# One decoder step on one core: high part of the first weight ahead of a layer-norm boundary, residual behind it, and low parts ahead of the pivot in the output projections

## The chip, the cores and the metric

The kernel runs on one core of one Trainium2 chip. The metric is the device time of one execution in microseconds (us); the figures are medians of several runs. Engines are named as in the profile: PE is TensorE, DVE is VectorE, ACT is ScalarE, POOL is GpSimd, SP is the engine that issues most DMAs.

## The reference

The reference is one inference step of a decoder with two layers for 256 prompt tokens and 8 samples of 4 tokens (288 columns in the kernel, width 1024). Each layer is a half-step SwiGLU feed-forward, a token mixer (gated linear attention, GLA, in layer 0; dilated attention over a shared key/value cache in layer 1), and a second half-step feed-forward. Each of the six sub-layers ends in the same way:

```python
def modulate(x, shift, scale):
    return x * (1.0 + scale[:, None, :]) + shift[:, None, :]

def post_norm(x, y, gate, g, b):
    return layer_norm(ALPHA * x + (1.0 + gate[:, None, :]) * y, g, b)
```

The result of `post_norm` is used twice: modulated it is the input of the next projection, and times `ALPHA` it is the residual that the next `post_norm` adds. Shifts, scales and gates come from a product with the large weight `w_ada`.

## The kernel before, in words

**Products.** Activations lie with the width on partitions, as 8 chunks of 128 x 288. Every large product is made from three matmuls on values that are split into a high and a low part (`mm3`: hi by xh on L531, hi by xl on L532, lo by xh on L533). The tiles `xh` and `xl` are the split activation, `hi` and `lo` the split weight; in the key/value projection the activation is called `kh` and `kl`, and between the two halves of a feed-forward `hh` and `hl`.

**Weights.** The class `Stream` loads pieces of 512 KB in the fixed order of `job_list` by SP's queue into 11 buffers `raw`. A weight of 1024 x 256 is two pieces, called parts here. Each part is split when it is asked for (`part`, `split_part`): ACT copies it to `hi` (L177) and DVE subtracts to get `lo` (L179). `take` prepares one job more than it returns, `more(n)` prepares n further parts. Jobs of kind `ada` are the pieces of `w_ada`; `fill` runs them on PE (L450, with the transposes L466) between other work. `weave` spreads a list of ada jobs among weights: `lead` weights come first, and the ada jobs are spread over the rest of the first `span`.

**What sets the order.** A tile scheduler orders each engine's instructions, except that those given to `pin` keep their written order in a chain for each engine. Engines run their queue in order. The splits, the instructions of a boundary and the statistics are pinned, the residual is not.

**A boundary** is the work between two sub-layers. I write (l, s) for the one after sub-layer s of layer l; there are five, (0,0), (0,1), (0,2), (1,0) and (1,1), around 272, 472, 714, 1014 and 1334 us of the trace. First come the layer-norm statistics (`stats`, L617 to L645): sums over partitions by matmuls with `ones` (L623, L627), then DVE's variance and ACT's root. `spread` (L651) brings the factor to all partitions. Then `post_norm` goes over the chunks c = 0 to 7: DVE takes off the mean (`center`, L668; for c up to 2 inside `stats` and `spread`), `scaled` makes the modulated value `xm` on DVE (L758 for the prompt, L763 and L764 for the samples), ACT rounds it to `xh` (L760, L765), and one chunk later DVE makes `xl` (L767, L769). After c = 2 comes `S.more(1)`: one part of the weight that follows is split there, with `hi` on ACT and `lo` on DVE. PE runs `project_chunkwise` behind it: for each chunk the matmuls of four PSUM banks, as soon as that chunk's `xh` and `xl` are there; PE's order is fixed and has ada matmuls (L450) between the chunks.

**The residual** (`Post.residual`) is a generator: for each chunk DVE makes `ax` from `z` with a factor and `rstd` (L676), and POOL adds a bias (L678). It yields after every second chunk, and its caller decides in the text where the next two are emitted: in `ffn` ahead of step i = 1 to 5, in `gla` all that is left ahead of `wk`, in the dilated attention behind `post_norm`. Since L676 is not pinned, the scheduler places it: in the built program all eight stand within the boundary's chunks on DVE.

**The output projections** (`out_proj`, weights `wo` of layer 0 and `wob` of layer 1) take four weights of two chunks each. The first two weights give chunks 0 to 3 together. `Post.sublayer` makes `z` from the product, the gate and the residual (L570, L573, L575). With `late` = 4 a rough mean, the pivot (tile `lnpiv`, L588, from chunks 0 and 1), is subtracted: from `z` of chunks 0 to 3 by DVE (L602), and from the residual `ax` of chunks 4 to 7 by POOL (L595). `add` sums up `z` (L664, DVE here) and its squares (L665, POOL). Chunks 4 to 7 follow from weights 2 and 3; `S.more(3)` ahead of weight 3 splits three further parts.

**Rotation.** Behind boundary (1,0) stands the query projection (`wq` of layer 1), each of whose products ends in a rotation: ACT copies the PSUM bank in four quarters to `xm` (L1294), DVE multiplies out of the bank (L1295, tile `lnsq`; after it the bank is free), POOL multiplies `xm` (L1296), DVE adds both (L1298). There are four PSUM banks `pa` for all products.

## Time and profile before

| | |
|---|---|
| median of 3 runs | 1561.36 us (1559.15 to 1568.56) |
| profiled execution | 1566.59 us, its span 1564.5 us |
| mean granted TensorE clock | 0.98 |
| busy: PE, DVE, ACT, POOL | 95%, 59%, 46%, 14% of the span |
| chain that ended last: PE, DVE, ACT | 83%, 9%, 3% |

A row of the timeline gives start, duration, engine, line, operation, output<-inputs with their shape, and a count where neighbours are put together; in brackets stands the time that the engine was idle just before and what ended it. A row of the waits gives the waiting engine, tile and line, what it waited for, the total, how many times, and the longest. Starts of neighbouring instructions lie closer than their durations, since they overlap in the engine's pipeline; what an instruction takes from its queue is the distance to the next start.

### The profile page before, as it was taken

The page shows a single profiled execution, that of the slowest core. Times are in us where ns is not written, and L with a number is a line of the kernel's source. Part 1 is how long each engine was busy: PE and PEld are TensorE (multiplying, and loading weights), DVE is VectorE, ACT ScalarE, POOL GpSimd, SP SyncE. Part 2 cuts the span into 40 slices and gives each one's busy share as a digit, 9 for nine tenths or more (in the row PEclk, how much of TensorE's full clock was granted, in tenths as well). Part 3 has the DMA queues.
Part 4 walks back from the last instruction along what each step waited for, and adds up shares of the span by engine and source line. Part 5 has one row for each costly group of instructions (what it writes and reads, how often), then busy time and mean ns, then how long its engine had stood idle before and what let it go on. Part 6 is the DMA issues. An engine that isn't in the chain of part 4 may idle for free.

```text
span 1564.5 us, 31623 instructions
## 1 busy us (share of the span) xinstructions
PE 1487.1 (95%) x12706; PEld 1336.2 (85%) x12706; DVE 927.6 (59%) x2020; ACT 715.7 (46%) x1178; POOL 217.2 (14%) x312
## 2 busy tenths in 40 slices
PE   6999999999899999998999999999999989899996
PEld 4999998799778999998899999898766638899995
DVE  3644545596786444448745444675775667755455
ACT  2443434755744444346444433486543343444432
POOL 0000031201522000224100003232301002200001
PEclk8999999999999999999999999999998989999998
DMA  9977685636856767864566676767687997555520
GB/s 300 321 228 241 213 273 160 214 99 199 293 190 217 233 216 236 299 209 152 179 206 204 202 239 204 250 195 246 226 303 278 348 329 256 193 162 162 175 82 31
DMA packets 238420, 342.67 MB, mean 219 GB/s; under 512 B 12471, under 2 KB 201985, under 8 KB 238274
## 3 DMA queue, kind: packets, MB, share of 16 engines
q1 hardware_dynamic: 235810, 333.34, 64.7%
q0 software_dynamic: 2048, 7.14, 1.2%
q8 instruction: 99, 1.62, 0.4%
q14 instruction: 47, 0.39, 0.1%
q10 hardware_dynamic: 416, 0.17, 0.0%
HBM read 332.36 MB, written 8.26 MB: 218 GB/s over the span
## 4 chain that ended last, share of the span: by engine, by line
PE 83%; DVE 9%; ACT 3%; issue 2%; DMA 1%; POOL 0%; SPq 0%; DVEq 0%; ACTq 0%; POOLq 0%
PE pa L531 21%; PE pa L532 21%; PE pa L533 21%; PE pd L450 4%; PE pb L1381 4%; PE pa L1384 3%; PE pa L1381 2%; DVE lo L179 1%; PE pa L1042 1%; ACT pe L1407 1%; DVE xm L758 1%; DVE ax L676 1%; DMA xp<-in_x_prompt_dram 1%; ACT hi L177 0%; DVE lnacc L664 0%
## 5 line engine op out<-in xcount | busy, mean ns | idle before, releaser
L532 PE MATMUL pa<-xl,hi 128*128 128x288 f32 x1860 | 551.6, 298 | 6.8 <-DVE xl L769 6.8
L179 DVE TENSOR_TENSOR lo<-raw,hi 128x1024 fp32r<-128x1024 f32 x350 | 421.0, 1211 | 221.3 <-ACT hi L177 220.5
L533 PE MATMUL pa<-xh,lo 128*128 128x288 f32 x1860 | 547.6, 296 | 3.7 <-DVE lo L179 3.7
L531 PE MATMUL pa<-xh,hi 128*128 128x288 f32 x1860 | 543.5, 299 | 1.2 <-DVE lnsq L1295 0.8
L177 ACT ACTIVATE hi<-raw 128x1024 fp32r<-128x1024 f32 x350 | 358.7, 1035 | 260.6 <-PE pa L532 218.3
L532 PEld LDWEIGHTS pa<-xl,hi 128*128 128x128 f32 x1860 | 351.9, 189 | 14.0 <-DVE xl L769 9.4
L531 PEld LDWEIGHTS pa<-xh,hi 128*128 128x128 f32 x1860 | 347.9, 189 | 13.5 <-issue 10.0
L533 PEld LDWEIGHTS pa<-xh,lo 128*128 128x128 f32 x1860 | 351.7, 189 | 4.3 <-DVE lo L179 4.2
L531 PE MATMUL pa<-hh,hi 128*128 128x288 f32 x704 | 209.9, 298 | 0.0
L533 PE MATMUL pa<-hh,lo 128*128 128x288 f32 x704 | 208.1, 296 | 0.0
L532 PE MATMUL pa<-hl,hi 128*128 128x288 f32 x704 | 208.1, 296 | 0.0
L874 DVE TENSOR_TENSOR sa<-pa,sa 128x288 f32<-128x288 f32 x88 | 39.7, 454 | 179.9 <-PE pa L533 175.2
L531 PEld LDWEIGHTS pa<-hh,hi 128*128 128x128 f32 x704 | 132.6, 188 | 4.3 <-issue 2.9
L532 PEld LDWEIGHTS pa<-hl,hi 128*128 128x128 f32 x704 | 132.4, 188 | 0.2
L533 PEld LDWEIGHTS pa<-hh,lo 128*128 128x128 f32 x704 | 132.4, 188 | 0.1
L875 ACT ACTIVATE hh<-sa 128x288 fp32r<-128x288 f32 x88 | 38.7, 445 | 134.0 <-DVE sa L874 131.1
L873 ACT ACTIVATE sa<-pa 128x288 f32<-128x288 f32 x88 | 34.9, 401 | 93.6 <-PE pa L533 93.5
L450 PE MATMUL pd<-raw,cT 128*32 128x256 f32 x1008 | 73.3, 385 | 1.5 <-DMA raw<-in_w_ada_dram 1.4
L593 POOL TENSOR_TENSOR z<-z,lnpiv 128x288 f32<-128x288 f32 x6 | 4.7, 801 | 482.7 <-ACT lnpiv L588 482.7
L1384 PEld LDWEIGHTS pa<-ident,raw 128*128 128x128 f32 x448 | 49.7, 144 | 20.4 <-issue 9.4
L678 POOL TENSOR_SCALAR ax<-ax,lnba 128x288 f32<-128x288 f32 x40 | 54.9, 1376 | 71.3 <-DVE xm L764 69.4
L1384 PE MATMUL pa<-ident,raw 128*128 128x128 f32 x448 | 58.4, 282 | 5.4 <-ACT kt L1512 5.4
(380 smaller groups left out, 1761.4 us busy)
## 6 DMA issues: line engine op xcount, KB each, us to landing
raw<-in_w_ffn_up_dram SPq DMA_DIRECT2D x172, 512.0 KB, 4.8
raw<-in_w_ada_dram SPq DMA_DIRECT2D x110, 512.0 KB, 5.2
raw<-in_w_ffn_down_dram SPq DMA_DIRECT2D x80, 512.0 KB, 4.6
raw<-in_cache_k_dram SPq DMA_DIRECT2D x56, 512.0 KB, 6.7
raw<-in_cache_v_dram SPq DMA_DIRECT2D x56, 512.0 KB, 7.3
raw<-in_w_in_a_dram SPq DMA_DIRECT2D x24, 512.0 KB, 4.0
raw<-in_w_q_b_dram SPq DMA_DIRECT2D x24, 512.0 KB, 4.5
raw<-in_w_ada_dram SPq DMA_DIRECT2D x32, 256.0 KB, 5.8
```

The costliest lines, as they stand in the source:

```text
L177: self.pin("act", self.nc.scalar.activation(hv, src, AF.Copy))
L179: self.pin(low, eng.tensor_tensor(out=lo, in0=src, in1=hv.bitcast(F32), op=ALU.subtract))
L450: T.matmul(ps[32 * q:32 * q + 32, :], lhsT=cT[:, k, :], rhs=raw[kk][:, 256 * q:256 * q + 256], start=(k == 0), stop=(k == DC - 1), tile_po ...
L531: ins = [T.matmul(ps, lhsT=whi, rhs=xhi, start=first, stop=False), T.matmul(ps, lhsT=whi, rhs=xlo, start=False, stop=False), T.matmul(ps, ...
L532: T.matmul(ps, lhsT=whi, rhs=xlo, start=False, stop=False),
L533: T.matmul(ps, lhsT=wlo, rhs=xhi, start=False, stop=last)]
L678: G.tensor_scalar(out=ax[:, c, :], in0=ax[:, c, :], scalar1=bb_[:, c:c + 1], scalar2=None, op0=ALU.add)
L873: A.activation(sa, pa[:, 0:NT], AF.Silu)
L874: V.tensor_tensor(out=sa, in0=pu[:, 0:NT], in1=sa, op=ALU.mult)
L875: A.activation(hh[:, m, :], sa, AF.Copy)
L1381: pin("pe", T.matmul(*a, **k))
L1384: pin("pe", T.transpose(*a))
```

## The change

There are four parts.

First, `Stream.begin` splits one part in two steps: `hi` is emitted ahead of the first chunk of a boundary, and `lo` where `S.more(1)` stood, after c = 2. For that `split_part` returns the second step as a function.

Second, the residual's DVE instruction is pinned, so that it stays where the text emits it. In `ffn` that is ahead of steps 1 to 5. In `gla` the residual goes from ahead of `wk` to the four `wv` weights, two chunks at each. At (1,0) it is emitted behind `post_norm`, in one go.

Third, in the output projections `catch_up` does the pivot work of all chunks on DVE, for `z` of chunks 0 to 3 and for `ax` of chunks 4 to 7, and it is emitted when the third weight has been taken, which has its second low part split by then. POOL keeps no pivot work there.

Fourth, in the query projection of layer 1 the ada jobs start two weights later (`lead` 6 in place of 4) and are spread over the first 11 weights.

```diff
 class Stream:
-        self.split_part(self.split.setdefault(i, Weight()), self.jobs[i], self.raw.pop(x), f"{x}", low)
-        self.freed.add(x)
-        self.release()
-        return True
+        rest = self.split_part(self.split.setdefault(i, Weight()), self.jobs[i], self.raw.pop(x), f"{x}", low)
+
+        def end():
+            rest()
+            self.freed.add(x)
+            self.release()
+            return True
+
+        return end if low is None else end()
...
         self.pin("act", self.nc.scalar.activation(hv, src, AF.Copy))
-        eng = self.nc.vector if low == "dve" else self.nc.gpsimd
-        self.pin(low, eng.tensor_tensor(out=lo, in0=src, in1=hv.bitcast(F32), op=ALU.subtract))
         w.append([y.rearrange("p k (m c) -> p m k c", c=min(P, cols)) for y in (hv, lo)])
+
+        def rest():
+            self.pin("dve", self.nc.vector.tensor_tensor(out=lo, in0=src, in1=hv.bitcast(F32), op=ALU.subtract))
+
+        return rest
...
+    def begin(self):
+
+        self.pump()
+        end = self.part(None) if self.np < len(self.parts) else None
+        return end or (lambda: None)
...
-    jobs += weave(wq, adas((1, 6))[x:] + adas((1, 7)), lead=4) + ca + wob + adas((1, 8))[2:]
+    jobs += weave(wq, adas((1, 6))[x:] + adas((1, 7)), lead=6, span=11) + ca + wob + adas((1, 8))[2:]
...
 class Post:
-                    for q in range(self.late, DC):
-                        G.tensor_tensor(out=ax[:, q, :], in0=ax[:, q, :], in1=self.pivot, op=ALU.subtract)
+                    if self.late == 2:
+                        for q in range(2, DC):
+                            G.tensor_tensor(out=ax[:, q, :], in0=ax[:, q, :], in1=self.pivot, op=ALU.subtract)
...
             elif c < self.late:
-                if c == self.late - 1:
-                    for q in range(self.late):
-                        V.tensor_tensor(out=z[:, q, :], in0=z[:, q, :], in1=self.pivot, op=ALU.subtract)
-                        self.add(q)
+                pass
...
+        def catch_up(self):
+
+            for q in range(self.late):
+                V.tensor_tensor(out=z[:, q, :], in0=z[:, q, :], in1=self.pivot, op=ALU.subtract)
+                V.tensor_tensor(out=ax[:, self.late + q, :], in0=ax[:, self.late + q, :], in1=self.pivot, op=ALU.subtract)
+                self.add(q)
...
             for c in range(DC):
-                V.scalar_tensor_tensor(out=ax[:, c, :], in0=z[:, c, :], scalar=ga[:, c:c + 1], in1=rstd, op0=ALU.mult,
-                                       op1=ALU.mult)
+                pin("dve", V.scalar_tensor_tensor(out=ax[:, c, :], in0=z[:, c, :], scalar=ga[:, c:c + 1], in1=rstd,
+                                                  op0=ALU.mult, op1=ALU.mult))
...
     def post_norm(post, l, s, nxt):
         last, rs = None, None
+        low = S.begin()
         for c in range(DC):
...
             if c == 2:
-                S.more(1)
+                low()
...
     def out_proj(kind, g, xh, xl, tiles):
         for i in range(2, 4):
             w_ = S.take((kind, i))
+            if i == 2:
+                post.catch_up()
             if i == 3:
                 S.more(3)
...
     def gla(xh, xl, residual):
         qk("wq", qT, DK ** -0.5)
         for t in range(3):
             gates(t)
-        for _ in residual:
-            pass
         qk("wk", kT, 1.0)
...
         for i in range(4):
             w_ = S.take(("wv", i))
+            next(residual)
             for m in range(2):
                 p_ = bankA()
                 project(p_, w_, m, xh, xl)
```

The line numbers shift by 7 to 21: the residual is L695 and L697 after the change (L676 and L678 before), `lo` is L186 (L179), `center` L687 (L668), `xm` L777, L782 and L783 (L758, L763, L764), `xl` L786 and L788 (L767, L769), the rotation L1316, L1317 and L1319 (L1295, L1296, L1298), the pivot's subtraction L672 and L673 (L602, L595), and the sum L683 (L664).

The first place is DVE in boundary (0,1), from the split of a weight part behind chunk 2 on. Before, it reads:

```order
L179 TENSOR_TENSOR lo_5130<-raw_4858,hi_5129 128x1024
L668 TENSOR_TENSOR z<-z,pb_5004 128x288
L758 SCALAR_TENSOR_TENSOR xm_5136<-z,affs_4681,pb_5052 128x256
L763 TENSOR_TENSOR xm_5136<-z,rsS_5107 128x32
L676 SCALAR_TENSOR_TENSOR ax<-z,lnga_5309,lnacc_5103 128x288
L764 TENSOR_TENSOR xm_5136<-xm_5136,affb_4682 128x32
L767 SCALAR_TENSOR_TENSOR xl_5043<-xm_5121,affb_4682,xh_5042 128x256
```

Now it reads:

```order
L186 TENSOR_TENSOR lo_5105<-raw_4836,hi_5104 128x1024
L687 TENSOR_TENSOR z<-z,pb_5004 128x288
L777 SCALAR_TENSOR_TENSOR xm_5136<-z,affs_4681,pb_5052 128x256
L782 TENSOR_TENSOR xm_5136<-z,rsS_5110 128x32
L485 TENSOR_TENSOR mods<-pb_5609,bT 128x4x9
L783 TENSOR_TENSOR xm_5136<-xm_5136,affb_4682 128x32
L786 SCALAR_TENSOR_TENSOR xl_5043<-xm_5124,affb_4682,xh_5042 128x256
```

The residual's `ax` is gone from every chunk of the boundary, and a small ada instruction (L485) that stood ahead of `lo` now stands behind it. All eight `ax` stand behind the last `xl`, among the next feed-forward's steps.

The second place is DVE in the first output projection, from the third weight's first `lo` on (its second one is `lo_4861` before and `lo_4839` now). Before:

```order
L179 TENSOR_TENSOR lo_4855<-raw_4462,hi_4854 128x1024
L575 TENSOR_TENSOR z<-z,ax 128x32
L602 TENSOR_TENSOR z<-z,lnpiv_4822 128x288 x3
L664 TENSOR_TENSOR lnacc_4824<-z 128x288
L602 TENSOR_TENSOR z<-z,lnpiv_4822 128x288
L664 TENSOR_TENSOR lnacc_4824<-lnacc_4824,z 128x288
L179 TENSOR_TENSOR lo_4861<-raw_4544,hi_4860 128x1024
```

Now:

```order
L186 TENSOR_TENSOR lo_4833<-raw_4462,hi_4832 128x1024
L589 TENSOR_TENSOR z<-z,ax 128x32
L186 TENSOR_TENSOR lo_4839<-raw_4544,hi_4838 128x1024
L672 TENSOR_TENSOR z<-z,lnpiv_4822 128x288
L673 TENSOR_TENSOR ax<-ax,lnpiv_4822 128x288
L672 TENSOR_TENSOR z<-z,lnpiv_4822 128x288
L673 TENSOR_TENSOR ax<-ax,lnpiv_4822 128x288
L683 TENSOR_TENSOR lnacc_4824<-z 128x288
```

The second `lo` has gone ahead of six instructions, and the subtraction from `ax` has come to DVE from POOL.

The third place is DVE and POOL behind the last chunk of boundary (1,0). On DVE, before:

```order
L767 SCALAR_TENSOR_TENSOR xl_11005<-xm_11130,affb_10854,xh_11004 128x256
L769 TENSOR_TENSOR xl_11005<-xm_11130,xh_11004 128x32
L673 TENSOR_SCALAR lnga_15482<-gT 128x8
L674 TENSOR_SCALAR lnba_15483<-gT 128x8
L179 TENSOR_TENSOR lo_11162<-raw_10786,hi_11161 128x1024
L179 TENSOR_TENSOR lo_11168<-raw_10840,hi_11167 128x1024
L1295 TENSOR_TENSOR lnsq_11294<-pa_11173,ropeq_11143 128x288
```

On DVE, now:

```order
L786 SCALAR_TENSOR_TENSOR xl_11005<-xm_11130,affb_10854,xh_11004 128x256
L788 TENSOR_TENSOR xl_11005<-xm_11130,xh_11004 128x32
L186 TENSOR_TENSOR lo_11162<-raw_10786,hi_11161 128x1024
L186 TENSOR_TENSOR lo_11168<-raw_10840,hi_11167 128x1024
L695 SCALAR_TENSOR_TENSOR ax<-z,lnga_11273,lnacc_11061 128x288 x8
L1316 TENSOR_TENSOR lnsq_11294<-pa_11173,ropeq_11143 128x288
```

On POOL, now (before, all eight of the residual's stand in a row ahead of the first rotation):

```order
L1317 TENSOR_TENSOR xm_11293<-xm_11293,ropeq_11143 128x288
L697 TENSOR_SCALAR ax<-ax,lnba_11274 128x288 x2
L1317 TENSOR_TENSOR xm_11303<-xm_11303,ropeq_11143 128x288
L697 TENSOR_SCALAR ax<-ax,lnba_11274 128x288 x6
L1317 TENSOR_TENSOR xm_11313<-xm_11313,ropeq_11143 128x288
L1317 TENSOR_TENSOR xm_11323<-xm_11323,ropeq_11143 128x288
```

Here the residual is not interleaved with anything: all eight stand in one block on DVE between the low parts and the first rotation, and on POOL six of them stand ahead of the third rotation's product.

More of the change, by code (lines that the diff above doesn't have):

```diff
@@ L192, in prep, with more @@
             pass
-    def more(self, n, low="dve"):
+    def more(self, n):
         self.pump()
-        while n and self.np < len(self.parts) and self.part(low):
+        while n and self.np < len(self.parts) and self.part():
             n -= 1
+    def begin(self):
+        self.pump()
+        end = self.part(None) if self.np < len(self.parts) else None
+        return end or (lambda: None)
     def fill(self, limit=None):
@@ L848, in first_group @@
             for i in range(2):
-                S.split_part(w[i], jfirst[i], wfirst[i][:, k0:k0 + 4, :], f"f{i}{k0}")
+                S.split_part(w[i], jfirst[i], wfirst[i][:, k0:k0 + 4, :], f"f{i}{k0}")()
             if k0 == 0:
```

## The prediction

> **What bounds the kernel now.** I read the page first, for the engine that sets the time:
>
> ```profile
> span 1564.5 us, 31623 instructions
> PE 1487.1 (95%) x12706; PEld 1336.2 (85%) x12706; DVE 927.6 (59%) x2020; ACT 715.7 (46%) x1178; POOL 217.2 (14%) x312
> ```
>
> PE is busy for 95%, and the change neither adds nor removes a matmul. So all that it can win is time in which PE waits, and all that it can lose is a new wait of PE. Next I read the waits with PE as the engine, and kept the rows at the places that the change touches:
>
> ```profile
> PE pa L532 <- DVE xl L769: 6.8, 10, 2.2
> PE pa L533 <- DVE lo L179: 4.2, 3, 1.9
> PE pa L532 <- DVE kl L769: 2.8, 2, 2.0
> PE pb L623 <- DVE z L575: 2.6, 2, 1.3
> PE pa L531 <- DVE lnsq L1295: 1.9, 2, 1.2
> PE pd L450 <- DMA raw<-in_w_ada_dram: 1.4, 2, 0.7
> ```
>
> All but the last are waits for DVE: xl and kl in the boundaries, lo and z in the output projections, lnsq at the first rotation behind a boundary. The six rows add up to 19.7 us. That is the size of the whole stake, 1.3% of the span. Last I read the timeline at each of the places, for the order in which DVE came to be late.
>
> **Boundaries.** These are DVE's rows in boundary (0,1):
>
> ```profile
> 471.30 1.22 DVE L179 TENSOR_TENSOR lo<-raw,hi 128x1024 fp32r<-128x1024 f32 x1
> 472.43 0.45 DVE L668 TENSOR_TENSOR z<-z,pb 128x288 f32<-128x288 f32 x1
> 473.42 0.51 DVE L676 SCALAR_TENSOR_TENSOR ax<-z,lnga,lnacc 128x288 f32<-128x288 f32 x1
> 473.84 0.19 DVE L764 TENSOR_TENSOR xm<-xm,affb 128x32 f32<-128x32 f32 x1
> 474.44 0.45 DVE L668 TENSOR_TENSOR z<-z,pb 128x288 f32<-128x288 f32 x1
> 482.88 0.45 DVE L769 TENSOR_TENSOR xl<-xm,xh 128x32 fp32r<-128x32 f32 x1
> ```
>
> DVE needs 2.01 us for a chunk (472.43 to 474.44) without any idle time, and the residual's L676 takes 0.42 of it (473.42 to 473.84). Eight of them are 3.4 us, and three stand ahead of the `lo` of 471.30. PE's rows for the same stretch, and its longest waits in the other boundaries:
>
> ```profile
> 272.32 0.40 PE L551 MATMUL pa<-xl,hi 128*128 128x288 f32 x1 [0.45 <-DVE xl L769]
> 278.27 0.40 PE L532 MATMUL pa<-xl,hi 128*128 128x288 f32 x1 [0.96 <-DVE xl L769]
> ...
> 474.58 0.40 PE L532 MATMUL pa<-xl,hi 128*128 128x288 f32 x1 [2.15 <-DVE xl L769]
> 478.96 0.40 PE L532 MATMUL pa<-xl,hi 128*128 128x288 f32 x1
> 483.63 0.40 PE L532 MATMUL pa<-xl,hi 128*128 128x288 f32 x1
> ...
> 712.77 0.40 PE L532 MATMUL pa<-kl,hi 128*128 128x288 f32 x1 [0.79 <-DVE kl L769]
> 716.59 0.61 PE L532 MATMUL pa<-kl,hi 128*128 128x288 f32 x1 [1.96 <-DVE kl L769]
> ...
> 1332.39 0.40 PE L532 MATMUL pa<-xl,hi 128*128 128x288 f32 x1 [0.81 <-DVE xl L769]
> 1336.20 0.40 PE L532 MATMUL pa<-xl,hi 128*128 128x288 f32 x1 [1.96 <-DVE xl L769]
> ```
>
> In (0,1) PE waits 2.15 us at chunk 3, and DVE's last xl, ready at 483.33, comes 0.3 us before PE takes it at 483.63. Without the residual DVE is 1.3 us earlier at chunk 3 (three L676) and 3.4 earlier at the end. What is left of the wait at chunk 3 is 0.9; but the chunks behind it then come at 1.6 us each (2.01 less 0.42), and PE needs more than that. So the least gain is 1.3 (three L676 ahead of the wait) and the most 3.4 (all eight). I take 2.6, as the waits that PE shows in this stretch are hardly larger.
>
> In (0,0) and (0,2) the first part adds its own piece. There DVE waited for the high half:
>
> ```profile
> 274.97 1.23 DVE L179 TENSOR_TENSOR lo<-raw,hi 128x1024 fp32r<-128x1024 f32 x1 [0.57 <-ACT hi L177]
> ```
>
> ACT's copy now stands ahead of the first xh, in time that ACT spends waiting for xm. That takes 0.57 from DVE's path, and with three L676 DVE is 1.8 us earlier at chunk 3. In (0,0) the shown waits are 0.45 and 0.96, together 1.4. I take 1.4 (least 0.8, most 2.4). In (0,2) they are 0.79 and 1.96 and a smaller one. I take 2.6 (least 1.6, most 3.2). In (1,1) they are 0.81 and 1.96. I take 2.2 (least 1.3, most 2.8). Cover for the moved residual in the three boundaries that lead into feed-forward steps or into the keys and values is DVE's own idle time:
>
> ```profile
> sum 50.00, PE 50.00 PEld 48.57 DVE 24.40 ACT 22.59 POOL 0.00; mean PE 10.00 PEld 9.71 DVE 4.88 ACT 4.52 POOL 0.00
> ```
>
> This is the sum over 490 to 540 us in windows of 10 us, in the feed-forward behind (0,1): DVE is busy for half of it, and the eight add 3.4 us of 50. There I cost them at nothing; with the cover gone they would cost those 3.4 us. Boundary sum: 1.4 + 2.6 + 2.6 + 2.2 = 8.8 us.
>
> **Output projections.** Rows of DVE, then of POOL, then of PE in the first one:
>
> ```profile
> 444.18 3.08 DVE L602 TENSOR_TENSOR z<-z,lnpiv 128x288 f32<-128x288 f32 x3
> 448.16 0.45 DVE L602 TENSOR_TENSOR z<-z,lnpiv 128x288 f32<-128x288 f32 x1
> 449.52 1.81 DVE L179 TENSOR_TENSOR lo<-raw,hi 128x1024 fp32r<-128x1024 f32 x1
> ```
>
> ```profile
> 443.35 3.60 POOL L595 TENSOR_TENSOR ax<-ax,lnpiv 128x288 f32<-128x288 f32 x4 [13.32 <-ACT lnpiv L588]
> ```
>
> ```profile
> 451.39 0.40 PE L533 MATMUL pa<-xh,lo 128*128 128x288 f32 x1 [1.89 <-DVE lo L179]
> 457.92 0.75 PE L623 MATMUL pb<-z,ones 128*128 128x288 f32 x2 [1.28 <-DVE z L575]
> ```
>
> DVE makes the second `lo` of weight 3 only at 449.52, behind the pivot work, and PE stands for it for 1.89 us. The pivot work is slow because POOL runs beside it: three L602 take 3.08 us, 1.03 each, beside POOL's L595 (443.35 to 446.95), and the fourth, outside that, 0.45. With `lo` ahead of all this the wait of 1.89 goes. DVE gets four subtractions from POOL, 4 x 0.45 = 1.8 us when alone, and saves about 3 x 0.58 = 1.7 on L602. So its pivot work is as long as before, and it no longer has PE waiting behind it. PE then arrives 1.89 earlier at the statistics. Their wait for the last z (1.28) would stay if DVE were the later one there, and shrink as the statistics' nine ada matmuls stand ahead of it on PE now. Least gain 1.9 (the lo wait alone), most 3.2 (both waits). I take 2.6, between them. The second output projection shows the same pair in the waits (twice L533 with 1.9, twice L623 with 1.3), so the term is 2 x 2.6 = 5.2 us.
>
> **GLA.** The residual of (0,0) goes into the value projection:
>
> ```profile
> 340.00:350.00 10.00, 10.00 (x100) 8.82 (x98) 9.81 (x21) 5.58 (x10) 0.00 (x0) 1.00 0.19 54
> sum 60.00, PE 60.00 PEld 54.53 DVE 55.64 ACT 32.06 POOL 0.38; mean PE 10.00 PEld 9.09 DVE 9.27 ACT 5.34 POOL 0.06
> ```
>
> From 310 to 370 us DVE has 4.4 us of idle time in 60 (in one window 0.2 in 10), and 3.4 us come in. DVE is not late for PE there before (PE is never idle), but the banks that it empties have little slack. Least cost 0 (all of it fits), most 3.4 (none does). I take 1.0.
>
> **Boundary (1,0) and the rotation.** Rows of DVE, POOL and PE:
>
> ```profile
> 1023.52 2.36 DVE L179 TENSOR_TENSOR lo<-raw,hi 128x1024 fp32r<-128x1024 f32 x2 [0.38 <-ACT hi L177]
> 1026.13 0.46 DVE L1295 TENSOR_TENSOR lnsq<-pa,ropeq 128x288 f32<-128x288 f32 x1 [0.25 <-ACT xm L1294]
> 1034.98 0.46 DVE L1295 TENSOR_TENSOR lnsq<-pa,ropeq 128x288 f32<-128x288 f32 x1
> 1037.73 0.46 DVE L1295 TENSOR_TENSOR lnsq<-pa,ropeq 128x288 f32<-128x288 f32 x1
> ```
>
> ```profile
> 271.77 3.73 POOL L678 TENSOR_SCALAR ax<-ax,lnba 128x288 f32<-128x288 f32 x3 [8.19 <-DVE xm L764]
> 1030.66 0.81 POOL L1296 TENSOR_TENSOR xm<-xm,ropeq 128x288 f32<-128x288 f32 x1 [2.00 <-ACT xm L1294]
> ```
>
> ```profile
> 1026.64 0.40 PE L531 MATMUL pa<-xh,hi 128*128 128x288 f32 x1 [0.76 <-DVE lnsq L1295]
> ```
>
> In the chunks DVE wins 3.4 us and PE its two waits for ada data (1.4 in the waits; the ada jobs now start two weights later). Then the block of eight, 3.4 us, stands between the two lo and the first rotation's L1295, which frees PE's bank. So L1295 comes at about 1026 as before, and what PE won in the chunks it waits here. Behind that POOL is the later one. Its six L678 in a row at 1.24 us (3.73 for three) are 7.4 us ahead of the third rotation's product, which was made at 1030.66. From my own walk through the queues (first product at 1024, two L678 and the second product until 1028.4, six L678 until 1035.8) the third now ends at 1036.6, five us later. DVE's queue stands behind it: the fourth L1295, and the fifth with the lo of the next weight. PE has the banks of the first three rotations by then; three products are at least 8 us of work (rotations stand 2.75 us apart, 1034.98 to 1037.73), until 1035 or 1036. So I estimate that it stands for about 1 us for the fourth bank and 1 us for the next lo. Least cost -1.4 (ada waits gone, the queue absorbs the rest), most +5 (the whole delay of the third product). I take +2.
>
> **Sum.** -8.8 - 5.2 + 1.0 + 2.0 = -11.0 us. Against the profiled execution's own time of 1566.59 us that is 1555.6. That execution was 5.2 above the median of the three runs, 1561.36, so on the median's scale it is 1550.4 us, 0.7% faster. A measurement of this kernel can tell about 1%, 15.6 us, from no change.
>
> **Rivals.**
>
> *All waits go.* If the chunks run at PE's pace, the statistics too, and neither GLA nor the rotation costs anything, the boundaries give 11.8 (3.4 + 3.2 + 2.8 + 2.4), the output projections 6.4, and the ada waits 1.4: 19.6 us, 1541.8. For it speaks that DVE's relief is larger than the waits in three of the boundaries; against it the block of eight ahead of the rotation, whose order is fixed.
>
> *The residual is only moved.* If GLA's DVE takes all 3.4 us onto PE's path, the rotation costs 5 and the boundaries give their least (1.3 + 0.8 + 1.6 + 1.3 = 5.0) with 3.8 in the output projections: -0.4 us, 1561.0. For it speaks the window with 9.81 of 10; against it that the kernel shows PE waiting for exactly the instructions that come earlier.
>
> *DVE and POOL block each other, and it is slower.* This is the case on the other side. It is one mechanism: a residual pair is 0.42 us on DVE and then one L678 on POOL, and if DVE's instructions with two SBUF inputs stand still while POOL runs L678, each pair costs DVE 0.42 + 1.24 = 1.7 us. In GLA that is 13.3 us for eight against 4.4 idle, a loss of 8.9; behind (1,0) it is 1.24 x 8 = 9.9 more on DVE in front of the rotations and the lo. With +18.8 in place of my +3.0 the sum is +4.8: 1566.2. It decides from the point where eight pairs cost DVE more than the 14.0 that I gain elsewhere. For it speaks that L602 took 1.03 beside POOL's L595; against it DVE's `lo` of 274.97, which has two SBUF inputs, lay beside the third of POOL's L678 (271.77 to 275.50) and took 1.23, as 1.22 without it at 471.30. So the row nearest to the case says no.
>
> [...]
>
> **How the numbers follow.** My forecast, the waits partly gone: 0.60. All waits go: 0.19. Only moved: 0.14. Blocked: 0.07. The time is that of the forecast, 1550.4. The range goes from 1542, the first rival, to 1561, the second; it leaves the third out and the outer half of the first. Faster by over 1% (under 1545.7) is most of the first rival and a small tail of the forecast: 0.22. Slower by over 1% (over 1577) would take the third with more than I priced: 0.03. Between: 0.75.
>
> **What would show it.** In the waits of the changed kernel the rows of L533 for lo at the two output projections should be gone, and those for xl and kl down from 9.6 us to under 3. DVE's chunk in a boundary should take 1.6 us, not 2.01. Behind (1,0) POOL's third rotation product should come at least 3 us later behind the first L1295 than before (1026.13 to 1030.66), with a wait of PE near it for L1316. The prediction is wrong if PE's idle sum goes down by more than 16 us or by less than 5, if L695 and L697 lengthen DVE's instructions in GLA, or if a wait for ACT takes the place of xl, above all in (1,1), where ACT has two high halves to make behind the chunks.

## The result and the profile after

The changed kernel takes 1553.14 us (median of 8 runs, 1550.3 to 1555.05) against 1561.78 us of the kernel before, measured beside it (8 runs, 1559.15 to 1568.56). The ratio is 0.9941 with a 95% interval of 0.9929 to 0.9954: 0.6% faster. The forecast was 1550.4 us, 11.0 less than before, in a range from 1542 to 1561; measured by the medians, it is 8.6 us less. The profiled execution took 1555.05 us, 1.9 above its median, where the one of before was 4.8 above its own, so the two profiles lie 2.9 us further apart than the medians.

The page of the changed kernel has PE busy for the same share:

```profile
span 1553.3 us, 31613 instructions
PE 1481.3 (95%) x12706; PEld 1333.5 (86%) x12706; DVE 924.3 (60%) x2028; ACT 714.4 (46%) x1180; POOL 213.5 (14%) x304
```

Its waits, with PE as the engine, at the places that the change touches (waiting tile and line, releaser, total, count, longest):

```profile
PE pd L464 <- DMA raw<-in_w_ada_dram: 4.3, 3, 2.7
PE pb L635 <- DVE z L589: 3.5, 2, 1.8
...
PE pa L545 <- DVE lnsq L1316: 2.2, 2, 1.2
PE pa L546 <- DVE xl L788: 1.9, 2, 1.0
...
PE pa L547 <- DVE lo L186: 1.7, 3, 0.9
...
PE pa L546 <- DVE kl L788: 1.0, 1, 1.0
```

The waits for xl and kl fell from 9.6 to 2.9 us, those for lo from 4.2 to 1.7 (and the 1.7 stand elsewhere, behind (1,0) and in the key/value projection). Three rows grew: the ada data from 1.4 to 4.3, the statistics' wait for z from 2.6 to 3.5, and a little the wait for the bank (`lnsq`), from 1.9 to 2.2. Together the six rows go from 19.7 to 14.6 us, while the span lost 11.2. So half of the gain is not in these rows. By the two pages PE's idle time (span less busy time) fell by 5.4 us, from 77.4 to 72.0, and its busy time for the same 12706 matmuls by 5.8, from 1487.1 to 1481.3: the other half is PE's rate.

To see where it lies I matched the third matmul of each product (L533 before, L547 now; 2728 in each trace, and in the same order) one by one and took the difference of their starts. The differences between two points tell what a stage won or lost. Minus is faster; points are in us of the trace of before:

| stage | from, to | measured | forecast |
|---|---|---|---|
| start | 0, 261.70 | -0.33 | 0 |
| boundary (0,0) | 261.70, 288.46 | -2.56 | -1.4 |
| GLA | 288.46, 422.14 | -0.92 | +1.0 |
| output projection of layer 0 | 422.14, 470.79 | -1.65 | -2.6 |
| boundary (0,1), from chunk 2 on | 470.79, 485.06 | -2.27 | -2.6 |
| feed-forward | 485.06, 698.44 | +0.75 | 0 |
| boundary (0,2) | 698.44, 723.09 | -3.21 | -2.6 |
| keys and values, start of the feed-forward | 723.09, 770.92 | +1.44 | 0 |
| boundary (1,0), query projection | 995.04, 1098.82 | +5.77 | +2.0 |
| attention over the cache, first half of `wob` | 1098.82, 1310.38 | -4.38 | 0 |
| second half of `wob`, statistics | 1310.38, 1332.62 | -1.53 | -2.6 |
| boundary (1,1) | 1332.62, 1348.00 | -2.13 | -2.2 |
| sum, with the stages in between, up to the last product | | -11.0 | -11.0 |

The sum is what I forecast for the profiled executions, but not its parts: (1,0) cost three times as much, and the attention, which the change does not touch, gave 4.4 back (the last section shows where they come from).

In boundary (0,1) DVE's chunk takes 1.70 to 1.71 us now (starts of `center`), where it took 2.01, and PE's wait of 2.15 is 0.88:

```profile
467.83 0.45 DVE L687 TENSOR_TENSOR z<-z,pb 128x288 f32<-128x288 f32 x1
469.54 0.45 DVE L687 TENSOR_TENSOR z<-z,pb 128x288 f32<-128x288 f32 x1
471.24 0.45 DVE L687 TENSOR_TENSOR z<-z,pb 128x288 f32<-128x288 f32 x1
```

```profile
467.97 0.40 PE L546 MATMUL pa<-xl,hi 128*128 128x288 f32 x1 [0.88 <-DVE xl L788]
```

In the first output projection the pivot work of 11 instructions takes 0.37 us for each (440.68 to 441.05). POOL has nothing to do there until 443.52, and the last of them take as long beside its sum of squares (L684, 443.52 to 445.50). But the two low parts ahead of chunk 6 take 1.8 us each, and the statistics wait:

```profile
440.68 0.45 DVE L672 TENSOR_TENSOR z<-z,lnpiv 128x288 f32<-128x288 f32 x1
441.05 0.45 DVE L673 TENSOR_TENSOR ax<-ax,lnpiv 128x288 f32<-128x288 f32 x1
...
449.06 3.57 DVE L186 TENSOR_TENSOR lo<-raw,hi 128x1024 fp32r<-128x1024 f32 x2
452.55 0.47 DVE L584 SCALAR_TENSOR_TENSOR z<-pa,gate,ax 128x256 f32<-128x256 f32 x1
```

```profile
453.67 0.75 PE L635 MATMUL pb<-z,ones 128*128 128x288 f32 x2 [1.80 <-DVE z L589]
```

Behind (1,0) it is as the order said: two and then six residual additions stand in POOL's queue among the rotations' products, and DVE stands for the third product.

```profile
1017.44 0.80 POOL L1317 TENSOR_TENSOR xm<-xm,ropeq 128x288 f32<-128x288 f32 x1 [27.83 <-ACT xm L1315]
1018.22 1.99 POOL L697 TENSOR_SCALAR ax<-ax,lnba 128x288 f32<-128x288 f32 x2
1020.18 0.80 POOL L1317 TENSOR_TENSOR xm<-xm,ropeq 128x288 f32<-128x288 f32 x1
1020.96 7.33 POOL L697 TENSOR_SCALAR ax<-ax,lnba 128x288 f32<-128x288 f32 x6
1028.26 1.55 POOL L1317 TENSOR_TENSOR xm<-xm,ropeq 128x288 f32<-128x288 f32 x2
```

```profile
1013.28 3.52 DVE L695 SCALAR_TENSOR_TENSOR ax<-z,lnga,lnacc 128x288 f32<-128x288 f32 x8
...
1029.09 1.01 DVE L1319 TENSOR_TENSOR z<-lnsq,xm 128x256 f32<-128x256 f32 x1 [4.62 <-POOL xm L1317]
```

PE's waits there (ada data in front, then the bank, then a low part):

```profile
1004.06 0.63 PE L464 MATMUL pd<-raw,cT 128*32 128x256 f32 x4 [2.68 <-DMA raw<-in_w_ada_dram]
...
1017.87 0.64 PE L464 MATMUL pd<-raw,cT 128*32 128x256 f32 x8 [0.99 <-DMA raw<-in_w_ada_dram]
1030.62 0.40 PE L545 MATMUL pa<-xh,hi 128*128 128x288 f32 x1 [1.15 <-DVE lnsq L1316]
1037.41 0.40 PE L547 MATMUL pa<-xh,lo 128*128 128x288 f32 x1 [0.91 <-DVE lo L186]
```

The rest is not in any wait, but in PE's rate. In the key/value projection two short waits stand, and behind them the distance from one matmul to the next goes from 0.13 to 0.24 us (753.01 to 753.16, then 753.40 and 753.64):

```profile
751.25 0.40 PE L545 MATMUL pa<-kh,hi 128*128 128x288 f32 x1 [0.91 <-ACT hi L182]
...
752.51 0.40 PE L547 MATMUL pa<-kh,lo 128*128 128x288 f32 x1 [0.46 <-DVE lo L186]
...
753.01 0.35 PE L547 MATMUL pa<-kh,lo 128*128 128x288 f32 x1
753.16 0.45 PE L545 MATMUL pa<-kh,hi 128*128 128x288 f32 x1
753.40 0.45 PE L546 MATMUL pa<-kl,hi 128*128 128x288 f32 x1
753.64 0.45 PE L547 MATMUL pa<-kh,lo 128*128 128x288 f32 x1
```

The waits are not new. In the trace of before they stand at the same two instructions with the same lengths, but no half rate follows there (granted clock 1.00 from 762.2 to 766.7 us):

```profile
761.51 0.40 PE L531 MATMUL pa<-kh,hi 128*128 128x288 f32 x1 [0.91 <-ACT hi L177]
...
762.77 0.40 PE L533 MATMUL pa<-kh,lo 128*128 128x288 f32 x1 [0.46 <-DVE lo L179]
```

### The profile page after: what moved, and what is told of

Read it like the earlier page. It is cut to its first block, busy times and chain, and to the rows that moved or that the text cites. A ratio compares the mean times of both kernels' runs of the same rounds, so it can differ in the third digit from the quotient of the medians.

```text
span 1553.3 us, 31613 instructions
## 1 busy us (share of the span) xinstructions
PE 1481.3 (95%) x12706; PEld 1333.5 (86%) x12706; DVE 924.3 (60%) x2028; ACT 714.4 (46%) x1180; POOL 213.5 (14%) x304
## 4 chain that ended last, share of the span: by engine, by line
PE 85%; DVE 6%; ACT 4%; issue 2%; DMA 2%; POOL 1%; SPq 0%; DVEq 0%; ACTq 0%; POOLq 0%
PE pa L545 22%; PE pa L546 22%; PE pa L547 22%; PE pd L464 4%; PE pb L1402 4%; PE pa L1405 3%; PE pa L1402 2%; DMA raw<-in_w_ada_dram 1%; PE pa L1062 1%; DVE lo L186 1%; ACT pe L1428 1%; ACT xm L1315 1%; DVE xm L777 1%; DMA xp<-in_x_prompt_dram 1%; PE pb L635 1%
## 5 line engine op out<-in xcount | busy, mean ns | idle before, releaser
L186 DVE TENSOR_TENSOR lo<-raw,hi 128x1024 fp32r<-128x1024 f32 x350 | 420.0, 1208 | 221.6 <-ACT hi L182 221.5
L547 PE MATMUL pa<-xh,lo 128*128 128x288 f32 x1860 | 547.2, 295 | 1.2 <-DVE lo L186 1.2
L182 ACT ACTIVATE hi<-raw 128x1024 fp32r<-128x1024 f32 x350 | 358.5, 1035 | 258.8 <-PE pa L546 214.8
L547 PEld LDWEIGHTS pa<-xh,lo 128*128 128x128 f32 x1860 | 351.1, 189 | 1.8 <-DVE lo L186 1.7
L547 PE MATMUL pa<-hh,lo 128*128 128x288 f32 x704 | 208.1, 296 | 0.0
L547 PEld LDWEIGHTS pa<-hh,lo 128*128 128x128 f32 x704 | 132.4, 188 | 0.1
L697 POOL TENSOR_SCALAR ax<-ax,lnba 128x288 f32<-128x288 f32 x40 | 58.1, 1462 | 203.3 <-DVE ax L695 203.1
L464 PE MATMUL pd<-raw,cT 128*32 128x256 f32 x1008 | 74.3, 386 | 4.8 <-DMA raw<-in_w_ada_dram 4.3
L1315 ACT ACTIVATE xm<-pa 32x288 f32<-32x288 f32 x128 | 51.5, 402 | 20.8 <-issue 6.4
```

Of the source, the lines that this page charges most:

```text
L182: self.pin("act", self.nc.scalar.activation(hv, src, AF.Copy))
L186: self.pin("dve", self.nc.vector.tensor_tensor(out=lo, in0=src, in1=hv.bitcast(F32), op=ALU.subtract))
L464: T.matmul(ps[32 * q:32 * q + 32, :], lhsT=cT[:, k, :], rhs=raw[kk][:, 256 * q:256 * q + 256], start=(k == 0), stop=(k == DC - 1), tile_po ...
L547: T.matmul(ps, lhsT=wlo, rhs=xhi, start=False, stop=last)]
L697: G.tensor_scalar(out=ax[:, c, :], in0=ax[:, c, :], scalar1=bb_[:, c:c + 1], scalar2=None, op0=ALU.add)
L1315: A.activation(sw[d:d + 32, :], ps[32 * q:32 * q + 32, 0:NT], AF.Copy)
```

## Experiments

All were timed beside the kernel before on the same chip; ratios are to that kernel. Waits and stages are those of each run's profiled execution.

### The fourth part undone

```diff
-    jobs += weave(wq, adas((1, 6))[x:] + adas((1, 7)), lead=6, span=11)
+    jobs += weave(wq, adas((1, 6))[x:] + adas((1, 7)), lead=4)
```

> The changed kernel with the fourth part undone: the ada jobs of the query projection start after four weights again. My theory: the changed kernel's waits of PE for ada data in boundary (1,0) (4.3 us in three, the longest 2.7) come from the two weight loads that now go ahead of them on SP's queue; with lead 4 they fall to about 1.5 us in all, and the matmuls that follow the 2.7 us wait at 0.24 us apart run at 0.13 again (1.5 us more). So 3 to 4 us faster than the changed kernel: ratio to before about 0.992. Rival: what (1,0) loses is set by the block of eight ahead of the rotation, and PE only waits there instead: ratio 0.994 as for the whole change, with the waits moved to lnsq and lo.

1554.09 us, ratio 0.9945 (0.9927 to 0.9963): the same as the whole change, the rival's number. The mechanism is half of mine. The wait of 2.68 us in the chunks is gone, so it does come from the two weight loads ahead of the ada loads. But a wait of 5.18 us for ada data stands further on, ahead of the product that follows the first four:

```profile
1018.76 1.06 PE L464 MATMUL pd<-raw,cT 128*32 128x256 f32 x2 [5.18 <-DMA raw<-in_w_ada_dram]
```

The load that it waits for was issued at 1013.21, and SP's queue had waited up to 5.0 us for DVE's `lo` to free a buffer. So the fourth part exchanges one late load for another.

### The residual of (1,0) spread over the rotations

```diff
-        def residual(self, l, s, rstd):
+        def residual(self, l, s, rstd, order=range(DC), each=2):
...
-            for c in range(DC):
+            for n, c in enumerate(order):
...
-                if c % 2:
+                if n % each == each - 1:
...
-        return rest, post.residual(l, s, rstd)
+        return rest, post.residual(l, s, rstd, *(((0, 3, 1, 4, 2, 5, 6, 7), 1) if (l, s) == (1, 0) else ()))
...
-        for _ in residual:
-            pass
         for x in range(4):
+            next(residual, None)
             rotate(ps[x], tab, q_out(x % 2, x // 2))
...
+                    next(residual, None)
                     rotate(p_, tab, q_out(2 * hq + m, g))
```

> The changed kernel, but the residual of (1,0) is emitted one chunk ahead of each rotation (chunks in the order 0, 3, 1, 4, 2, 5, 6, 7, since the rotations overwrite z in that order) in place of one block of eight. My theory: POOL's third rotation product then is not behind six residual additions, and the waits of PE for lnsq (1.15 us) and lo (0.6 and 0.9 us) behind (1,0) go: 2 to 3 us faster than the changed kernel, ratio about 0.9925. Rival: PE's lead at that point is used up by the late ada data ahead of it, so the block costs nothing: ratio 0.994.

1549.14 us, ratio 0.9919 (0.9896 to 0.9942), as I expected. DVE's longest wait for POOL's product is 0.70 us in place of 4.62, the wait for the bank is gone, and that for lo is 0.5. The stage of (1,0) costs 0.3 us in place of 5.8. 2.9 us of that come from the chunks ahead, where the wait for ada data was 1.26 us in place of 2.68 and no half rate followed (granted clock 1.00 from 1005 to 1010 us, against 0.66 in the changed kernel); the two orders do not differ there, so this part is not the edit's.

### Both

The two edits above together.

> Both edits together (lead 4 again, the residual of (1,0) one chunk ahead of each rotation). My theory: the two losses are at different places and add up, 5 to 7 us faster than the changed kernel, ratio 0.990 to 0.991. Rival: one covers the other, and the ratio is that of the better single edit, 0.992 to 0.9925.

1550.8 us, ratio 0.9926 (0.9907 to 0.9945): they do not add up, and here my theory falls. No ada wait is left, but one of 2.5 us for `lo`, with half rate behind it (granted clock 0.72 from 1035 to 1040 us). SP's queue waited up to 7.1 us there for DVE's `lo` to free one of the 11 buffers. I read this so: if the ada jobs come early, the weights come late. No run with more buffers tested it.

### Only POOL's order changed

DVE's block of eight stays; POOL's additions are emitted apart from it, one behind each rotation, and both are pinned.

```diff
+            for c in range(DC if apart else 0):
+                yield
+                pin("pool", G.tensor_scalar(out=ax[:, c, :], in0=ax[:, c, :], scalar1=bb_[:, c:c + 1], scalar2=None,
+                                            op0=ALU.add))
...
-        G.tensor_tensor(out=sw, in0=sw, in1=tab[:, 1, :], op=ALU.mult)
+        pin("pool", G.tensor_tensor(out=sw, in0=sw, in1=tab[:, 1, :], op=ALU.mult))
```

> The changed kernel with DVE's and PE's order untouched (the block of eight stays ahead of the first rotation of (1,0)), but on POOL one residual addition behind each rotation's product in place of two and then six in a row. My theory: what stops DVE for 4.6 us behind (1,0) is POOL's queue (third product behind six additions, 7.3 us), and not DVE's block of 3.5 us; so PE's waits for lnsq (1.15 us) and lo (0.6 and 0.9) there go or shrink to under 1 us together, as with the residual spread over both engines: about 2 us faster at that place than the changed kernel, ratio about 0.9925. Rival: the block itself is the delay, then these waits stay and the ratio is 0.994.

1551.94 us, ratio 0.9933 (0.9921 to 0.9945). The times alone do not tell the two theories apart; the trace does. DVE's wait for the third product is gone, and so are PE's waits of 1.15 and 0.91; from 1033.38 to 1041.35 us of the trace of before the changed kernel loses 3.0 us, this one none. So POOL's queue is the delay, and not DVE's block. The stage as a whole costs 0.95 us in place of 5.77; 1.6 us of that difference lie further ahead, up to 1030 us, where most of it is a half rate that follows the late ada data in the changed kernel and not here, and are not the edit's. DVE's longest waits for a product of POOL are now 0.8 and 0.9 us; the first of them:

```profile
1013.66 4.31 DVE L695 SCALAR_TENSOR_TENSOR ax<-z,lnga,lnacc 128x288 f32<-128x288 f32 x8
...
1025.01 0.42 DVE L1324 TENSOR_TENSOR z<-lnsq,xm 128x256 f32<-128x256 f32 x1 [0.78 <-POOL xm L1322]
```

### The residual not pinned

```diff
-                pin("dve", V.scalar_tensor_tensor(out=ax[:, c, :], in0=z[:, c, :], scalar=ga[:, c:c + 1], in1=rstd,
-                                                  op0=ALU.mult, op1=ALU.mult))
+                V.scalar_tensor_tensor(out=ax[:, c, :], in0=z[:, c, :], scalar=ga[:, c:c + 1], in1=rstd, op0=ALU.mult,
+                                       op1=ALU.mult)
```

> The changed kernel with the residual not pinned, so that the scheduler puts its eight instructions back among the chunks of each boundary (order of before), everything else as changed. My theory: the residual's 0.42 us for a chunk is the main part of what the boundaries win; DVE needs 2.0 us for a chunk again, the waits of PE for xl and kl come back to 5 us or more, and the time is 1557 to 1560, ratio 0.997 to 0.999. Rival: the gain comes from the high half ahead and from the output projections, and the residual was hidden: ratio 0.994 or better, as the loss behind (1,0) is gone too.

1555.67 us, ratio 0.9955 (0.994 to 0.9971), between the two. The waits for xl and kl come back to 8.9 us in these three rows, the first chunk's row (L565) included; the same rows of the changed kernel have 3.4:

```profile
PE pa L546 <- DVE xl L788: 4.8, 8, 1.3
...
PE pa L546 <- DVE kl L788: 2.6, 5, 1.3
...
PE pa L565 <- DVE xl L788: 1.5, 3, 0.9
```

By stages the pin is worth 1.9, 1.4, 2.3 and 1.5 us in (0,0), (0,1), (0,2) and (1,1), 7.0 in all, and costs 4.6 in (1,0), 0.75 in the feed-forward behind (0,1) (where ada matmuls moved) and 1.2 in the keys and values (the half rate shown above, which this execution does not have).

### The residual alone

The kernel before, with the same pin and GLA's place for the residual.

> The kernel before with the second part alone (the residual pinned behind the boundaries, in GLA at the value weights). My theory: the four boundaries (0,0), (0,1), (0,2), (1,1) win 1.5 to 2.3 us each, about 7 in all; the block of eight behind (1,0) loses 5 or more of them, with the wait for ada data there at 5 us as in the run with lead 4; so 0 to 3 us faster, ratio 0.998 to 1.000. Rival: the loss behind (1,0) belongs to the moved ada jobs and not to the block, then the ratio is 0.995 to 0.996.

1558.9 us, ratio 0.9979 (0.9969 to 0.9988), as I expected, with a wait for ada data of 3.4 us behind the block. By stages the four boundaries win 1.9, 1.6, 2.3 and 1.2 us, 7.1 in all, and (1,0) loses 5.75. So the loss at (1,0) does not need the moved ada jobs.

### The output projections alone

The kernel before, with `catch_up`, its call at the third weight, and the old pivot work taken out, as in the change.

> The kernel before with the third part of the change alone (both low parts of the third weight ahead of the pivot work, and that on DVE). My theory: the wait of PE for lo in the two output projections (1.89 and 1.85 us) goes, and 0.4 us of it comes back in the statistics' wait for z (1.28 to about 1.75), so 1.4 us at each: 1.5 to 3.5 us faster than before, ratio 0.998. Rival, as I predicted it: both waits shrink, 2.6 us at each, ratio 0.9965 or less.

1556.63 us, ratio 0.9968 (0.9955 to 0.9981), between the theories and nearer to the rival. The trace is as my theory has it: no wait for lo is left there, and the two for z are 1.79 and 1.74 us. The first output projection wins 1.5 us. The second one wins 0.45, as 0.6 us more of waiting for the first chunk's xl stands behind it (0.85 in place of 0.22). That is far less than the ratio says. Most of the profiled execution's gain lies in the attention (6.0 us), which this kernel does not change either; how much of the ratio is due to that stays open.

### The pivot back on POOL

```diff
-                V.tensor_tensor(out=ax[:, self.late + q, :], in0=ax[:, self.late + q, :], in1=self.pivot, op=ALU.subtract)
+                G.tensor_tensor(out=ax[:, self.late + q, :], in0=ax[:, self.late + q, :], in1=self.pivot, op=ALU.subtract)
```

> The changed kernel with the residual's pivot subtraction in the output projections (four instructions each) back on POOL, the low parts still ahead. My theory: DVE's L672 take about 1.0 us each again beside POOL's, against 0.37 for each of eight instructions now, so DVE's pivot work is as long either way, and no PE wait stands behind it: within 1 us at each output projection, ratio 0.993 to 0.9955. Rival: POOL, which then starts its sums of squares 3.6 us later, ends them later than chunk 7, and the statistics wait for it: 1 to 2 us lost at each, ratio 0.996.

1554.22 us, ratio 0.9956 (0.9943 to 0.997), which overlaps with the whole change. One of DVE's four subtractions (L672) takes 1.06 us and the other three take 2.41 together, against 0.45 each. A new wait stands ahead of the statistics, not for POOL's squares, as the rival had it, but for DVE's own sum, which the slower subtractions delay; it is 0.59 us, and 0.56 in the second projection:

```profile
451.29 0.75 PE L635 MATMUL pb<-lnacc,ones 128*128 128x288 f32 x2 [0.59 <-DVE lnacc L683]
453.74 0.75 PE L635 MATMUL pb<-z,ones 128*128 128x288 f32 x2 [1.70 <-DVE z L589]
```

So what matters most in the third part is that `lo` comes first; by the waits, that DVE takes the pivot is worth about 0.5 us at each projection (0.59 and 0.56 more for the sum, 0.1 and 0.05 less for z). The stages of this trace lose 2.3 and 0.6 us against the changed kernel, but a stretch of half rate (granted clock 0.50 from 455 to 460 us, 0.68 from 1315 to 1320), which the changed kernel's execution does not have, lies behind each of these waits.

### Without the first part

```diff
-        low = S.begin()
...
-                low()
+                S.more(1)
```

> The changed kernel without the first part (both halves of the boundary's weight part are made behind chunk 2 again). My theory: DVE waits 0.57 us for hi in (0,0) and (0,2), and a little in the others now that DVE comes earlier there, and PE's longest wait of each boundary grows by as much: 1 to 3 us slower than the changed kernel in all, ratio 0.995 to 0.996. Rival: DVE has slack there now without the residual, no difference, 0.994.

1557.13 us, ratio 0.997 (0.9958 to 0.9983): 0.3% slower than the changed kernel, somewhat more than I expected. Without the residual DVE reaches `lo` earlier, and `hi` is the later one in each of the four boundaries (DVE waits 0.82 us for it): PE's waits at chunk 3 are 1.50, 1.91 and 1.90 us in (0,1), (0,2) and (1,1), against 0.88, 0.98 and 0.98 in the changed kernel. The first part and the second add up. In (0,0), (0,1) and (1,1) together the run without the pin wins 2.25 us, the residual alone 4.8, and the whole change 7.0. ((0,2) is left out, since a half rate of before went in all three.)

### Two low parts behind chunk 7

The run with the residual spread over the rotations, and besides:

```diff
+            if self.low and c == DC - 1:
+                pin("dve", end)
...
+                for f in self.low:
+                    f()
                 self.stats(zc)
...
-                S.more(3)
+                S.more(1)
+                post.low = [S.begin() for _ in range(2)]
```

Here `end` is the last instruction that makes `z` of a chunk.

> The run with the residual of (1,0) spread over the rotations, and besides, in the output projections, two of the three low parts that stand ahead of chunks 6 and 7 on DVE put behind chunk 7, ahead of the variance. My theory: the statistics' wait of PE for z (1.78 and 1.74 us) is DVE's 3.6 us for those two low parts beside POOL's sums, and goes for the most part; the variance comes no later, as DVE waits 2.9 us ahead of it: 2 to 3.5 us faster than with the spread alone, ratio 0.990. Rival: the wait only moves behind the statistics, to the variance, and the ratio stays at 0.992.

1541.43 us, ratio 0.9866 (0.9847 to 0.9885), the lowest ratio of all and faster than expected. DVE's rows of the first output projection:

```profile
449.87 0.47 DVE L585 SCALAR_TENSOR_TENSOR z<-pa,gate,ax 128x256 f32<-128x256 f32 x1
...
451.44 0.19 DVE L590 TENSOR_TENSOR z<-z,ax 128x32 f32<-128x32 f32 x1
451.55 2.35 DVE L186 TENSOR_TENSOR lo<-raw,hi 128x1024 fp32r<-128x1024 f32 x2
454.04 0.23 DVE L658 TENSOR_TENSOR lnpiv<-pb,lnpiv 128x72 f32<-128x72 f32 x1
```

The two low parts take 2.35 us here, where POOL is busy for 1.41 us from 450 to 455 us, and 3.57 in the changed kernel, beside POOL's sums of squares (L684, until 451.54). The wait for z is gone, the variance (L658) does not wait for the low parts, and the boundary behind starts earlier. The first projection with its statistics wins 5.3 us in place of 1.65, the second one 5.4 in place of 1.5. This is 3.7 and 3.9 us more, about twice the wait for z. The scheduler has also moved PE's ada matmuls (L464): 18 stood between the statistics' sums in front of that wait (450.39 to 451.9 in the changed kernel), and here 26 stand behind the sums (453.53 to 455.42), until DVE's reciprocal (454.76, 0.60 us) of the root is done, which PE needs next. How the gain divides between the two was not tested.

### The key/value projection's second pair in halves, and all additions together

`rest` is made a generator, and its chunks 4 to 7 are emitted at the sixth weight; on top of the run with the spread, then also with the low parts behind.

```diff
                     next(step, None)
+                    if c == 3:
+                        yield
...
                 if i == 4:
-                    rest()
+                    half = rest()
+                if i in (4, 5):
+                    next(half, None)
```

> The run with the residual of (1,0) spread over the rotations, and besides, in the key/value projection, the second modulated pair (xh, xl of all eight chunks, made in one go at the fifth weight) made in two halves, so that ACT comes to the high half of the sixth weight earlier. My theory: PE's waits there for hi (0.91 us) and lo (0.46) cause the half rate that follows them (matmuls 0.24 us apart for about 3.5 us, mean granted clock 0.62 from 752 to 756.5), so that with the waits gone the half rate goes too: 2 to 3 us faster than with the spread alone, ratio about 0.990. Rival: the half rate comes at that time whatever PE did just before, then only the waits go, 1.4 us.

1549.67 us, ratio 0.9916 (0.9894 to 0.9937). In the profiled execution the waits of 0.91 and 0.46 and the half rate behind them are gone, 2.9 us with 1.0 us more won behind (the stage wins 2.4 where it lost 1.5); the timed runs show next to nothing of it.

> The three additions to the changed kernel together: the residual of (1,0) spread over the rotations, the key/value projection's second pair in two halves, and two of the three low parts behind chunk 7 in the output projections. My theory: they lie at different places and add up: 1.4 us of waits and up to 1.7 us of half rate less than with the spread and the low parts behind, 1538 to 1540 us, ratio 0.985. Rival: what the halves win is given back where the next weights' high parts come, as the run with the halves alone was not faster than the spread in the timed runs: ratio 0.9865.

1540.67 us, ratio 0.987 (0.9855 to 0.9884), the same as without the halves. So the times are the rival's in both, but the traces do not show that the gain is given back. Two things explain part of it. The half rate follows these two waits in only 4 of the 12 traces that have them (see the last section), so a median should hold little of it. And the waits alone, 1.4 us, are less than the intervals of these ratios can tell (2 to 3 us either way). The rest is open.

## Why the prediction was right, point by point

**What bounds.** PE's waits were the right place to look. The stake of 19.7 us was not the whole, though: the run with two low parts behind chunk 7 is 20.9 us faster than before (by its interval 18 to 24), and 6.1 us of the six rows' waits are still there. PE's rate is part of the time too.

**Boundaries.** Forecast 8.8, measured 10.2 (2.56 + 2.27 + 3.21 + 2.13). The mechanism held: the residual on DVE was the largest part, as the run without the pin and the run with the residual alone show. The size is partly luck: 0.75 of the 10.2 are ada matmuls that only moved behind (0,1), and up to 1.7 are half rate. The gains in (0,0) and (0,2) were at or above the most that I allowed; I had counted waits, and in (0,2) a stretch of half rate (716.6 to 720.0 us of the trace of before) went with the wait. DVE's chunk came down to 1.70, not to 1.6. I gave the first part a price only in (0,0) and (0,2); it has one in (0,1) and (1,1) too.

**Output projections.** Forecast 5.2, measured 3.2 with the statistics (1.65 + 1.53), less than my least. The step that failed is the one that had the statistics' wait shrink: it grew from 1.28 to 1.80, since three low parts still stood ahead of the last two chunks. The row of 3.57 us for two of them, and the run that moves them, show the true price.

**GLA.** Forecast +1.0, measured -0.9, and the sign is probably the clock's: the trace of before lost 3.4 us of full rate there to half rate, this one 1.7. The two runs that leave the residual out of this stage win 1.55 and 1.47 us there, so the eight instructions cost about 0.6. Most of them fit into the 4.4 us of idle time.

**(1,0).** Forecast +2.0, measured +5.8, above my most. POOL's queue was as I walked it (a third product 11 us behind the first, DVE standing for 4.6 us), and the waits for bank and lo were 1.15 and 0.32 + 0.91 for my 1 + 1. What failed is the sentence that PE wins its two waits for ada data there: they became three, 1.4 to 4.3 us, with half rate behind the longest (granted clock 0.50 from 1005.69 to 1009.11 us). In the run with lead 4 the wait came back at another place; a third place for those jobs was not tried.

**The other rivals.** That DVE and POOL block each other did not happen on DVE: L695 took 0.505 to 0.673 us in all 40 places, and the 14 `lo` (L186, two SBUF inputs) that started while an L697 was running, with 0.2 us or more of it to go, took 1.22 us at most, as elsewhere. POOL's took longer: two L697 took 4.07 us in GLA, beside a DVE that is 97% busy (58.08 of 60 us), where two take 1.99 behind (1,0):

```profile
310.47 4.07 POOL L697 TENSOR_SCALAR ax<-ax,lnba 128x288 f32<-128x288 f32 x2 [47.22 <-DVE ax L695]
```

The other three pairs in GLA took 3.01, 3.24 and 2.44 us. So POOL is slower beside this DVE; that DVE stands still until POOL is done, as this rival had it, is not what the trace shows where DVE starts second beside this form of POOL's.

**The sum** was right to the microsecond in the profiled executions, and that is luck: 3.8 us too little loss at (1,0), 2.0 too much gain in the output projections, against 1.4 more in the boundaries, 1.9 in GLA and 4.4 in the attention, and 1.9 lost in stages that I had put at nothing. On the medians 8.6 us were measured for the 11.0.

**The signs.** The rows of `lo` at the output projections are gone, xl and kl are under 3 us, and the third product came more than 3 us later, with a wait for L1316 near it. PE's idle time fell by 5.4 us, hardly above the 5 below which I had called the prediction wrong. No wait of PE for ACT took the place of xl in (1,1), and of the 28 DVE instructions that lie beside an L697 in GLA one (L1084) took 0.92 us, against a median of 0.69 for this line, and the others hardly longer than elsewhere.

## What to carry to other kernels

Work that nobody needs soon, in the loop of the engine that sets the pace, is worth moving (here 1.4 to 2.3 us at a boundary for 3.4 us of it); but follow every engine of the moved piece into the queue where it lands, since here six short additions on an idle engine held back the chain of two others (7.33 us for the six, 4.62 us of waiting on DVE). When a wait on one instruction is removed, look at what stands ahead of the next one: putting one low part ahead of the pivot won about 1.6 us at each output projection, and putting the next two behind the statistics' input won another 3.8. And match the same instructions in two traces, with the granted clock beside them, before adding up waits.

## What the hardware showed that I had not expected

In the middle of the program PE's rate halves for 3.4 us at a time, or twice that (granted clock 0.50 from 753.11 to 756.52 us in the changed kernel, from 296.73 to 303.54 in the kernel before), and it takes no long wait. In the changed kernel the waits ahead of it were 0.91 and 0.46 us; in the run with lead 4 the same instructions stand behind the same two waits, and nothing follows. Here is a window of 4.5 us for each (busy times with counts, then the granted clock, DMA share and GB/s), first the changed kernel, then the run with lead 4:

```profile
752.00:756.50 4.50, 4.04 (x19) 3.99 (x19) 4.05 (x5) 2.04 (x3) 0.00 (x0) 0.62 0.60 168
```

```profile
751.70:756.20 4.50, 4.04 (x31) 4.02 (x31) 4.02 (x5) 2.43 (x4) 0.00 (x0) 1.00 0.61 180
```

The one runs 19 matmuls, the other 31; 12 matmuls at 0.13 us are 1.6 us. In the trace of before the granted clock is below 1 from 1170 to 1195 and from 1270 to 1295 us. Summed up over windows of 5 us (one less the clock, times 5), that is 12.0 us of full rate lost in the attention and the start of `wob`; the changed kernel lost 5.1 there. This is enough for the 4.4 us that the attention seemed to give back. All the other traces agree: against the trace of before this stage wins more, the less full rate it loses, from 2.3 us in the run with lead 4 (8.5 lost) over 4.4 in the changed kernel to 7.3 in the run with two low parts behind chunk 7 (1.7 lost). So two profiled executions can differ by some microseconds for this alone, and a gain of that size in a stage that a change does not touch is not the change's. What halves the clock was not shown: the half rate followed 1.4 us of waiting in two pieces in some traces and not in others.

Whether the moment of the two waits decides it can be read from the traces. Twelve of the fourteen have the waits of 0.91 and 0.46 us in the key/value projection, and the half rate follows in four of them. Within each trace the changes of the granted clock, but for the first, lie on a grid of 3.413 us to within 0.01 us, and the grid lies elsewhere in each execution. Measured from the last line of the grid, the wait of 0.91 us begins at 0.64 to 0.78 us in those four, and at 0.03, 0.10 or from 1.40 us on in the other eight. In the four both waits end before the next line, and the half rate begins on it. In the two at 0.03 and 0.10 both waits lie between two lines of the grid too and nothing follows, so that alone is not enough. I read this afterwards, and no run tested it.
